# A two-layer latent trunk on one core: h summed in DRAM by the DMA, g stored from GpSimd, layer 0's gate columns computed in the first stage, and a new order of the loop's pieces

## The chip, the cores and the metric

The kernel runs on one core of one Trainium2 chip. The metric is the device time of one execution in microseconds, the median of three runs. A profile of one execution comes with each kernel; its times count from the first instruction.

## What is computed

Two residual layers over 1024 latent tokens and 256 context tokens, width 1024, in float32. Layer 0 is a bidirectional gated linear recurrence (RG-LRU) of width 1408, layer 1 a windowed attention. The change lies in layer 0:

```
def modulation(vec, w, b):
    m = jax.nn.silu(vec) @ w + b
    shift, scale, gate = jnp.split(m, 3, axis=-1)
...
    a = jnp.exp(log_a)
    b = jnp.sqrt(-jnp.expm1(2.0 * log_a)) * (i * uf)
...
    h_l = hl_dirs[0] + hl_dirs[1]
    y_l = (h_l * jax.nn.silu(g_l.astype(jnp.float32))).astype(n_l.dtype) @ w_out
...
        h_lat = h_lat + gt_l * y_l
```

Here u and g are the two halves of n @ w_in, u goes through a convolution over four tokens, r and i are sigmoids of products of u with 16 block matrices of 88x88 for each direction, and each direction is a linear scan over the tokens, with the context first. The two directions' h are added, multiplied by silu(g) and projected.

## The kernel before

Channels lie on partitions, the 1280 tokens in the free dimension, in three token tiles of 512, 512 and 256 (CH). Float32 products are made of three passes over a rounded part and a remainder (mm3, lines 76 to 78), so each operand is split in two: the rounded part mostly by ScalarE, the remainder mostly by VectorE.

The program fixes the order of every engine by hand (a manual schedule). Two tables of short names set it: `sorder` for the first stage (loads, norm, modulation, u of the first two channel tiles) and `order` for the loop over the rest. An entry such as `U3.1.0` is one half of the product of u tile 3 with token tile 1; each engine and each DMA queue runs its own entries in the table's order, and waits only where data or a buffer is missing.

The names in the loop: W loads half a weight tile, wh and wl split it; U and G are products for u and g (G over 11 tiles t, three token tiles, two halves of 12 matmuls); c1 and tp the convolution; ub copies blocks of u to 88 partitions, uh and ul split them; Q is the product for the gates of block b, in three parts of nine matmuls, into one PSUM tile `gtps`; sg its sigmoid into a tile M (two buffers); pc moves M's rows by DMA to the channel tiles R (for r) and I (for i), z = 0 forward and 1 reverse, four buffers each. Then, for each channel tile (chain) j and direction z: tn, ex and sq (tanh, exp, square root, ScalarE), iu, m1, m2 (VectorE), and sc, the scan, which writes over I. `ad` adds the two directions on VectorE (ch_add, line 524) and `hs` stores the sum to h_dr in DRAM (line 527). `ev` copies a G product from its bank (two banks) into the one buffer ev_g, and `gs` stores it to g_dr (line 612). All DMAs are issued by SyncE, in the table's order. GpSimd does next to nothing in the loop.

The last entries, once all gates are done, are the drain. Into it the program places loads for what follows: three tiles of h and g (og_load, lines 744 and 745), and gate columns of layer 0 (ada_w0g, 4 MB): ad_load, ad_mm (16 products of 32x512, line 551), ad_row (line 556) and ad_tr (four transposes, line 562, and the adds into gate0). Then the output projection runs (names c and wh_j, wl_j; GpSimd makes wl_j at line 70): it multiplies h by silu(g) in tiles (og_prep, line 750), which og_load keeps four ahead.

Of the kernel before, what the change touches and what calls it, by code (L numbers as in the profile page):

```python
# [8 lines left out]
F32 = mybir.dt.float32  # L9
# [26 lines left out]
def trunk(ctx: ExitStack, tc: tile.TileContext, I, out, dbg=None, stop=None):  # L36
# [155 lines left out]
    sel2 = px.tile([P, 2], F32, name="sel2")  # L192
    nbn = px.tile([P, KD], F32, name="nbn")
# [90 lines left out]
    def ada0_row(b):  # L284
        arow[b] = px.tile([P, 256], F32, tag="arow", name=f"arow0_{b}", bufs=1)
        act.copy(arow[b], aps[b][:, :256])
# [63 lines left out]
    dve.tensor_reduce(sel2, ident.rearrange("p (j r) -> p r j", j=4)[:, 0:2, :], op=ALU.add, axis=mybir.AxisListType.X)  # L350
    lam_b()
# [3 lines left out]
    def diag(i):  # L355
# [20 lines left out]
    uo = {i: [a[1] for f, a in sorder if f == "U" and a[0] == i] for i in range(3)}
    lasta = max(n for n, (f, _) in enumerate(sorder) if f == "am")
# [239 lines left out]
    def c_tap(k, x):  # L617
# [151 lines left out]
    def ogx(i, k):  # L769
# [811 lines left out]
```

## Time and profile before

| | us |
|---|---|
| runs before | 1262.64, 1263.79, 1263.93 |
| median | 1263.79 |
| the profiled execution | 1264.06 |
| its span, first to last instruction | 1262.2 |
| TensorE busy | 1186.7 (94%) |
| VectorE busy | 759.1 (60%) |
| ScalarE busy | 726.7 (58%) |
| GpSimd busy | 467.3 (37%) |

TensorE is busy nearly throughout. The span is not one stage: the first stage, the loop with its drain, the output projection, layer 1's products, its attention and its projection follow each other, and each has its own limit. A busy share says little on a change that lies in one of them; the stretch and its waits have to be read. Matmuls overlap, so the distance between two starts, not the duration of one, is what a matmul costs.

### The profile page before, as it was taken

To read this page: it belongs to the slowest core of one execution; us is meant where nothing else is said; L and a number is where in the kernel's file an instruction comes from. 1 tells how busy PE (TensorE), PEld (TensorE's weight loads), DVE (VectorE), ACT (ScalarE), POOL (GpSimd) and SP (SyncE) were. 2 spreads that over 40 slices of the span, in tenths; PEclk is the share of its full clock that TensorE was granted. 3 is DMA by queue.
4 is the path that set the end of the run, shared out by engine and by line. 5 is a ranking of instruction groups with operands and counts; after the bars stand their busy time and mean duration, and the time that the engine had idled before them with its cause. 6 is when DMAs were issued, how large, how long until landed. Compare 5 with 4: busy or idle time off the path is not lost. (4 is left out here: it accounts for less than half of the span.)

```text
span 1262.2 us, 18495 instructions
## 1 busy us (share of the span) xinstructions
PE 1186.7 (94%) x6702; PEld 975.9 (77%) x6702; DVE 759.1 (60%) x1185; ACT 726.7 (58%) x1163; POOL 467.3 (37%) x528
## 2 busy tenths in 40 slices
PE   8999999999987878889999999999999999999997
PEld 7788878878775756767788888777778887876787
DVE  3763958677686375643055735530069999996343
ACT  5656878677696465641022545631179999985212
POOL 3000000000000002454547545553248888898722
PEclk9999989999998889999999999999999999999998
DMA  9435565646555666968516457789482442211422
GB/s 351 157 90 165 159 188 156 166 125 187 137 160 149 174 241 218 328 210 290 180 55 226 168 173 226 219 246 321 137 260 65 169 142 89 85 34 43 142 84 68
DMA packets 96653, 214.02 MB, mean 170 GB/s; under 512 B 10290, under 2 KB 23986, under 8 KB 94514
## 3 DMA queue, kind: packets, MB, share of 16 engines
q1 hardware_dynamic: 96562, 212.84, 53.6%
q8 instruction: 53, 0.87, 0.3%
q14 instruction: 38, 0.31, 0.1%
HBM read 127.73 MB, written 49.02 MB: 140 GB/s over the span
## 5 line engine op out<-in xcount | busy, mean ns | idle before, releaser
L70 POOL TENSOR_TENSOR wl_j<-ws_j,wh_j 128x512 fp32r<-128x512 f32 (+1 forms) x94 | 127.4, 1359 | 461.6 <-ACT wh_j L717 447.0
L1182 DVE CUSTOM_DVE_ANT_0 p<-s,mask,snk 128x640 f32<-128x640 f32 (+1 forms) x128 | 106.7, 837 | 23.8 <-PE s L1171 23.5
L1202 POOL TENSOR_SCALAR p<-p,den 128x640 f32<-128x640 f32 (+1 forms) x128 | 98.6, 793 | 59.5 <-DVE den L1198 45.7
L76 PE MATMUL g<-n0h,wh 128*128 128x512 f32 (+1 forms) x264 | 99.3, 376 | 15.1 <-ACT ev_g L608 13.9
L1188 ACT ACTIVATE p<-p,nm 128x640 f32<-128x640 f32 (+1 forms) x128 | 102.7, 804 | 1.2 <-DVE nm L1182 1.1
L77 PE MATMUL g<-n0h,wl 128*128 128x512 f32 (+1 forms) x264 | 98.5, 373 | 0.0
L78 PE MATMUL g<-n0l,wh 128*128 128x512 f32 (+1 forms) x264 | 97.4, 369 | 0.0
L1214 PE MATMUL t<-ident,p 128*128 128x128 f32 x608 | 92.9, 276 | 2.6 <-DVE tl L1229 2.0
L1214 PEld LDWEIGHTS t<-ident,p 128*128 128x128 f32 x608 | 72.3, 141 | 27.3 <-DVE tl L1229 12.5
L76 PE MATMUL u<-n0h,wh 128*128 128x512 f32 (+1 forms) x240 | 87.0, 363 | 3.4 <-DVE uc L414 3.4
L77 PE MATMUL u<-n0h,wl 128*128 128x512 f32 (+1 forms) x240 | 85.9, 358 | 0.0
L78 PE MATMUL u<-n0l,wh 128*128 128x512 f32 (+1 forms) x240 | 85.5, 356 | 0.0
L1229 DVE TENSOR_TENSOR tl<-t,th 128x512 fp32r<-128x512 f32 x120 | 82.2, 687 | 1.9 <-ACT th L1221 1.1
L471 ACT ACTIVATE M<-gtps,pack 128x1280 f32<-128x1280 f32 (+1 forms) x48 | 63.7, 1327 | 29.6 <-PE gtps L78 26.2
L67 POOL TENSOR_SCALAR wh_j<-ws_j 128x512 fp32r<-128x512 f32 (+1 forms) x72 | 51.9, 720 | 70.7 <-DMA ws_j<-w_in1t 25.7
L1221 ACT CAST th<-t 128x512 fp32r<-128x512 f32 x120 | 70.4, 587 | 11.5 <-PE t L1214 7.8
L77 PE MATMUL c<-n0h,wl_j 128*128 128x512 f32 x192 | 69.9, 364 | 2.7 <-POOL wl_j L70 2.7
L76 PE MATMUL c<-n0h,wh_j 128*128 128x512 f32 x192 | 70.2, 366 | 2.0 <-ACT wh_j L717 2.0
L76 PEld LDWEIGHTS g<-n0h,wh 128*128 128x128 f32 x264 | 53.2, 201 | 24.2 <-ACT ev_g L608 15.8
L78 PE MATMUL c<-n0l,wh_j 128*128 128x512 f32 x192 | 68.9, 359 | 0.0
L76 PE MATMUL gtps<-uh,gh 88*128 88x512 f32 (+1 forms) x144 | 53.9, 374 | 14.5 <-ACT M L471 14.4
L1169 PE MATMUL s<-kst,qa 128*128 128x256 f32 x256 | 59.6, 314 | 4.1 <-DVE nm L1182 2.9
(447 smaller groups left out, 3429.6 us busy)
## 6 DMA issues: line engine op xcount, KB each, us to landing
qa<-x_dr SPq DMA_DIRECT2D x16, 1024.0 KB
aw<-ada_w SPq DMA_DIRECT2D x48, 256.0 KB
ws_j<-w_in1t SPq DMA_DIRECT2D x48, 256.0 KB
ws<-w_in0t SPq DMA_DIRECT2D x44, 256.0 KB
adaw<-ada_w0c SPq DMA_DIRECT2D x16, 512.0 KB
x_dr<-h_q SPq DMA_DIRECT2D x32, 256.0 KB
x_dr<-l_q SPq DMA_DIRECT2D x32, 256.0 KB
h_dr<-I SPq DMA_DIRECT2D x11, 640.0 KB
```

What stands on the lines that cost most here:

```text
L70: pool.tensor_tensor(d, a, b, op=ALU.subtract)
L76: pe.matmul(ps, wh, xh, start=first, stop=False)
L77: pe.matmul(ps, wl, xh, start=False, stop=False)
L78: pe.matmul(ps, wh, xl, start=False, stop=last)
L471: act.activation(t[:rows], d.pop(("ps", m))[:rows, :T], AF.Sigmoid, bias=gbias[:rows, b, m:m + 1])
L1169: pe.matmul(ps[:, 256:512], qp, kst[:, z, NL:], start=(z == 0), stop=(z == 1))
L1182: dve.tensor_tensor_reduce(p, ps[:, 256:256 + nk], msk, 1.0, snk[:, h:h + 1], ALU.add, ALU.min, d["nm"][:, hh:hh + 1])
L1188: act.activation(p, p, AF.Exp, bias=d["nm"][:, hh:hh + 1], scale=-1.0, accum_out=d["den"][:, hh:hh + 1])
L1202: pool.tensor_scalar(d["p"][hh], d["p"][hh], d["den"][:, hh:hh + 1], 1.0, op0=ALU.mult, op1=ALU.mult)
L1214: pe.transpose(tp[:, y * P:(y + 1) * P], d["p"][hh][:, x * P:(x + 1) * P], ident)
L1221: act.copy(d["h", i], d["t", i])
L1229: dve.tensor_tensor(d["l", i], d["t", i], d["h", i], op=ALU.subtract)
```

## The change

`ad` and `hs` go. In their place stand `hx`, a plain store of the reverse direction's I to h_dr, and `hy`, a DMA that adds the forward direction's I to the same rows of h_dr; both are issued by GpSimd, as are the g stores now. Gate columns of layer 0 are computed in the first stage: gd loads a 128x1024 part of ada_w0g, gm makes four of the 16 products, gr copies the rows, gt turns them into columns with a selection matrix (four products with four columns), gc adds the bias. The drain's ada pieces go, and six h and g tiles in place of three are loaded in it. Both tables are new; of each a line or two is shown.

```
+    sel4 = px.tile([P, 4], F32, name="sel4")
...
+    def gd(t):
+        w = araw["g", t] = pw.tile([P, 1024], F32, tag="adaw", name=f"adawg{t}", bufs=8)
+        nc.sync.dma_start(w, I["ada_w0g"][t * P:(t + 1) * P, :])
+
+    def gm(q):
+        if q == 0:
+            aps["g"] = gt("adapsg")
+        for a in range(2):
+            for h in range(2):
+                pe.matmul(aps["g"][64 * a + 32 * h:64 * a + 32 * h + 32], scc[:, 2 * q + a, :],
+                          araw["g", 2 * q + a][:, 512 * h:512 * h + 512], start=(q == 0), stop=(q == 3))
+
+    def g_row(_):
+        arow["g"] = px.tile([P, 512], F32, tag="arow", name="arowg", bufs=1)
+        act.copy(arow["g"], aps["g"])
+
+    def g_tr(_):
+        for c in range(4):
+            pe.matmul(aps["g"][:, 4 * c:4 * c + 4], arow["g"][:, c * P:(c + 1) * P], sel4, start=True, stop=True)
+
+    def g_col(_):
+        pc = aps["g"][:, 0:16].rearrange("p (c h r) -> p h c r", h=2, r=2)
+        for h in range(2):
+            hs = slice(4 * h, 4 * h + 4)
+            dve.tensor_tensor(gate0[:, hs, :], pc[:, h], ada_b0[:, 2 * KD:3 * KD].unsqueeze(2).to_broadcast([P, KD, 2])[:, hs], op=ALU.add)
...
-        ev0.0 l2.7 U2.2 U2.7 ev0.2 ev1.2
...
+        U2.2 wl2.0 ev0.1 U2.4 ev1.1 U2.0 h2.7 U2.1 wh2.1 l2.7 gr0 U2.7 wl2.1 gt0 ev1.2 ev0.2 gc0
...
-    lasta = max(n for n, (f, _) in enumerate(sorder) if f == "am")
+    lasta = max(n for n, (f, _) in enumerate(sorder) if f in ("am", "gm"))
...
-    def ch_add(j):
-        c = chn[j]
-        dve.tensor_tensor(c["I", 0], c["I", 0], c["I", 1], op=ALU.add)
-
-    def hstore(j):
-        nc.sync.dma_start(h_dr[j * P:(j + 1) * P, :], chn.pop(j)["I", 0])
+    def hstore1(j):
+        pool.dma_start(h_dr[j * P:(j + 1) * P, :], chn[j]["I", 1])
+
+    def hstore0(j):
+        pool.dma_start(h_dr[j * P:(j + 1) * P, :], chn.pop(j)["I", 0], accum_op=ALU.add)
...
-        nc.sync.dma_start(g_dr[t * P:(t + 1) * P, c0:c0 + n], evg.pop((t, i)))
+        pool.dma_start(g_dr[t * P:(t + 1) * P, c0:c0 + n], evg.pop((t, i)))
...
-        m110.1 ev9.1 G10.2.1 gs9.1 m210.1 G9.2.0 sc10.1 G9.2.1 ev10.2 gs10.2 ad10 hs10 ev9.2 gs9.2
...
+        m29.1 G9.2.1 ex10.0 sc9.1 sq10.0 hx9 ev9.2 m110.0 gs9.2 m210.0 sc10.0 hy10 ev10.2 gs10.2 hy9
...
-    hq0 = adE.enter_context(pl_(name="hq0", bufs=3, side="right"))
+    hq0 = adE.enter_context(pl_(name="hq0", bufs=6, side="right"))
...
-    og_load(0, 0)
-    ad_load(2)
-    og_load(0, 1)
-    ad_load(6)
-    og_load(0, 2)
-    lastg = [n for n, (f, _) in enumerate(order) if f == "G"][-4]
...
+    left = len(order) - lastu - 1
+    ogat = {lastu + 1 + (q + 1) * left // 8: q for q in range(6)}
     for n, (f, a) in enumerate(order[lastu + 1:], lastu + 1):
-        if n == lastg:
-            ad_mm(0)
-            ad_load(8)
+        if n in ogat:
+            og_load(0, ogat[n])
         loop[f](*a)
...
-    for q in range(1, 4):
-        ad_mm(q)
...
-    ogn = [3, 0]
+    ogn = [6, 0]
```

SyncE's queue where the gates of block 15 come, before (R1_10 is the reverse direction's R of chain 10, M15_0 the first part of block 15's gates, ev_g7_0 a G product):

```order
L485 DMA R1_10_3466<-M15_0_3449 88x1280
L485 DMA R0_10_3468<-M15_0_3449 40x1280
L612 DMA g_dr_61<-ev_g7_0_3473 128x512
L485 DMA R0_10_3468<-M15_1_3476 48x1280
L485 DMA I1_10_3494<-M15_1_3476 80x1280
L612 DMA g_dr_61<-ev_g7_1_3506 128x512
L485 DMA R1_9_3302<-M14_0_3524 48x1280
L485 DMA R1_10_3466<-M14_0_3524 40x1280
L485 DMA R0_9_3305<-M14_0_3524 40x1280
L172 DMA ws21_0_3556<-w_in0t 128x512
L612 DMA g_dr_61<-ev_g7_2_3558 128x256
```

and after:

```order
L515 DMA R1_10_3542<-M15_0_3510 88x1280
L515 DMA R0_10_3544<-M15_0_3510 40x1280
L515 DMA R0_10_3544<-M15_1_3588 48x1280
L515 DMA I1_10_3605<-M15_1_3588 80x1280
L515 DMA I1_10_3605<-M15_2_3635 8x1280
L515 DMA I0_10_3650<-M15_2_3635 88x1280
L172 DMA ws20_1_3662<-w_in0t 128x512
L172 DMA ws21_0_3666<-w_in0t 128x512
L515 DMA R1_9_3359<-M14_0_3669 48x1280
```

The three g stores between the pieces are gone from this queue, and block 15's last part stands ahead of block 14's first.

GpSimd's queue at the end of the loop, before (uc0 is the first convolution, wl_j0 the projection's first weight remainder):

```order
L268 TENSOR_SCALAR sp8_117<-lam_0_119 128x22
L406 TENSOR_SCALAR uc0_861<-ev0_665,pack_62 128x1280
L70 TENSOR_TENSOR wl_j0_3965<-ws_j0_3776,wh_j0_3964 128x512
L70 TENSOR_TENSOR wl_j1_3975<-ws_j1_3778,wh_j1_3974 128x512
L70 TENSOR_TENSOR wl_j2_4009<-ws_j2_3780,wh_j2_4008 128x512
```

and after (the DMA of I1 is the plain h store, that of I0 the accumulating one):

```order
L553 DMA h_dr_60<-I1_10_3605 128x1280
L641 DMA g_dr_61<-ev_g9_1_3913 128x512
L553 DMA h_dr_60<-I1_9_3393 128x1280
L641 DMA g_dr_61<-ev_g9_2_3961 128x256
L556 DMA h_dr_60<-I0_10_3650 128x1280
L641 DMA g_dr_61<-ev_g10_2_3969 128x256
L556 DMA h_dr_60<-I0_9_3438 128x1280
L70 TENSOR_TENSOR wl_j0_3984<-ws_j0_3843,wh_j0_3983 128x512
```

Where nothing stood between the first convolution and the projection there are now 55 stores, and the last of them stand ahead of wl_j0.

VectorE at the end of the drain, before (chains 9 and 10; t2 is the product's tile):

```order
L507 SCALAR_TENSOR_TENSOR t2_10_0_3774<-R0_10_3468,t2_10_0_3774 128x1280
L524 TENSOR_TENSOR I0_9_3388<-I0_9_3388,I1_9_3340 128x1280
L511 TENSOR_TENSOR t2_10_0_3774<-t2_10_0_3774,I0_10_3620 128x1280
L517 SCALAR_TENSOR_TENSOR I0_10_3620<-R0_10_3468,t2_10_0_3774 128x256
L518 SCALAR_TENSOR_TENSOR I0_10_3620<-R0_10_3468,I0_10_3620,t2_10_0_3774 128x1024
L507 SCALAR_TENSOR_TENSOR t2_10_1_3832<-R1_10_3466,t2_10_1_3832 128x1280
L511 TENSOR_TENSOR t2_10_1_3832<-t2_10_1_3832,I1_10_3494 128x1280
L520 SCALAR_TENSOR_TENSOR I1_10_3494<-R1_10_3466,t2_10_1_3832 128x1280
L524 TENSOR_TENSOR I0_10_3620<-I0_10_3620,I1_10_3494 128x1280
```

and after (oh0_0 is the projection's first h tile):

```order
L537 SCALAR_TENSOR_TENSOR t2_9_1_3889<-R1_9_3359,t2_9_1_3889 128x1280
L541 TENSOR_TENSOR t2_9_1_3889<-t2_9_1_3889,I1_9_3393 128x1280
L550 SCALAR_TENSOR_TENSOR I1_9_3393<-R1_9_3359,t2_9_1_3889 128x1280
L537 SCALAR_TENSOR_TENSOR t2_10_0_3934<-R0_10_3544,t2_10_0_3934 128x1280
L541 TENSOR_TENSOR t2_10_0_3934<-t2_10_0_3934,I0_10_3650 128x1280
L547 SCALAR_TENSOR_TENSOR I0_10_3650<-R0_10_3544,t2_10_0_3934 128x256
L548 SCALAR_TENSOR_TENSOR I0_10_3650<-R0_10_3544,I0_10_3650,t2_10_0_3934 128x1024
L778 TENSOR_TENSOR oh0_0_3852<-oh0_0_3852,sg0_0_3853 128x512
```

The two additions (L524) are gone, the forward direction of chain 10 is last, and the reverse direction of chain 9 stands right ahead of it.

## Rows read from the trace of the kernel before

**Rows 1.** Busy time by stretches: us, then PE, PEld, DVE, ACT, POOL, granted clock, DMA, GB/s.
```profile
140.00:160.00 20.00, 20.00 (x104) 17.11 (x103) 16.22 (x15) 19.11 (x18) 0.00 (x0) 1.00 0.57 164
...
400.00:420.00 20.00, 10.94 (x36) 8.43 (x34) 16.27 (x12) 10.46 (x10) 0.00 (x0) 0.74 0.20 52
...
520.00:540.00 20.00, 18.53 (x80) 14.46 (x78) 12.83 (x16) 12.47 (x23) 7.96 (x7) 1.00 0.97 360
```

**Rows 2.** Waits of SyncE's queue, 380 to 487 us: total, times, longest.
```profile
SPq L485 <- DVE I L520: 17.3, 1, 17.3
```

**Rows 3.** Timeline of SyncE's queue, 380 to 470 us: start, duration of the issues, line.
```profile
393.73 2.00 SPq L485 DMA_DIRECT2D I<-M  x3
413.06 3.68 SPq L485 DMA_DIRECT2D R<-M  x2
416.84 0.43 SPq L612 DMA_DIRECT2D g_dr<-ev_g  x1
...
462.19 7.49 SPq L612 DMA_DIRECT2D g_dr<-ev_g  x2
```

**Rows 4.** Timeline of TensorE: start, duration, operation, in brackets the idle time before.
```profile
395.52 0.39 PE L77 MATMUL g<-n0h,wl 128*128 128x512 f32 x1
395.74 0.39 PE L78 MATMUL g<-n0l,wh 128*128 128x512 f32 x1
...
407.08 0.80 PE L76 MATMUL gtps<-uh,gh 88*128 88x512 f32 x1 [5.79 <-ACT M L471]
...
408.53 0.63 PE L76 MATMUL gtps<-uh,gh 88*128 88x512 f32 x1
408.96 0.63 PE L77 MATMUL gtps<-uh,gl 88*128 88x512 f32 x1
...
421.54 0.58 PE L76 MATMUL g<-n0h,wh 128*128 128x256 f32 x1 [4.82 <-ACT ev_g L608]
...
440.49 0.28 PE L78 MATMUL gtps<-ublk,gh 88*96 88x256 f32 x1
...
493.21 0.77 PE L76 MATMUL c<-n0h,wh_j 128*128 128x512 f32 x1
```

**Rows 5.** Timeline of ScalarE, the copies of G products.
```profile
408.60 0.58 ACT L608 COPY ev_g<-g 128x512 f32<-128x512 f32 x1
...
420.90 0.59 ACT L608 COPY ev_g<-g 128x512 f32<-128x512 f32 x1 [8.84 <-DMA g_dr<-ev_g]
...
468.74 0.59 ACT L608 COPY ev_g<-g 128x512 f32<-128x512 f32 x1 [10.07 <-DMA g_dr<-ev_g]
```

**Rows 6.** VectorE's groups by shape, 380 to 488 us: busy, mean ns, idle before.
```profile
L511 DVE TENSOR_TENSOR t<-t,I 128x1280 f32<-128x1280 f32 x6 | 8.8, 1487 | 0.1
...
L520 DVE TENSOR_TENSOR_SCAN I<-R,t 128x1280 f32<-128x1280 f32 x3 | 8.5, 2818 | 0.0
L518 DVE TENSOR_TENSOR_SCAN I<-R,I,t 128x1024 f32<-128x1024 f32 x3 | 7.1, 2351 | 0.1
```

**Rows 7.** ScalarE's groups by shape, 380 to 488 us.
```profile
L495 ACT ACTIVATE R<-R,sp 128x1280 f32<-128x1280 f32 x6 | 8.1, 1362 | 0.1
...
L499 ACT ACTIVATE t<-t 128x1280 f32<-128x1280 f32 x6 | 7.7, 1276 | 0.1
...
L499 ACT ACT_TABLE_LOAD x5 | 6.4, 1283 | 0.1
```

**Rows 8.** Timeline of TensorE, the products for the gate columns.
```profile
477.86 1.07 PE L551 MATMUL adaps<-aw,scc 128*32 128x512 f32 x8
...
484.80 2.78 PE L551 MATMUL adaps<-aw,scc 128*32 128x512 f32 x24
```

**Rows 9.** Waits of TensorE, 493 to 620 us: total, times, longest.
```profile
PE c L77 <- POOL wl_j L70: 4.3, 5, 1.0
```

**Rows 10.** Waits of ScalarE, 487 to 560 us.
```profile
ACT sg L750 <- DMA sg<-g_dr: 18.4, 9, 3.5
```

**Rows 11.** Waits of TensorE in the loop up to 340 us.
```profile
PE gtps L76 <- ACT M L471: 7.1, 5, 2.4
```

More of the change, by code (lines that the diff above doesn't have):

```diff
@@ L284, in ada0_row @@
     def ada0_row(b):
-        arow[b] = px.tile([P, 256], F32, tag="arow", name=f"arow0_{b}", bufs=1)
+        arow[b] = px.tile([P, 512], F32, tag="arow", name=f"arow0_{b}", bufs=1)[:, :256]
         act.copy(arow[b], aps[b][:, :256])
@@ L350, in trunk @@
     dve.tensor_reduce(sel2, ident.rearrange("p (j r) -> p r j", j=4)[:, 0:2, :], op=ALU.add, axis=mybir.AxisListType.X)
+    dve.tensor_reduce(sel4.rearrange("p (h r) -> p h r", h=2),
+                      ident.rearrange("p (a h r) -> p h r a", a=2, h=2)[:, :, 0:2, :], op=ALU.add, axis=mybir.AxisListType.X)
     lam_b()
@@ new lines, in trunk @@
+        am3.0 y0.0 h1.0 U1.1 A5.0 wh1.1 l1.0 h0.0 am3.1 wl1.1 A4.1 U1.0 row3 l0.0 A2.1 tr3 am4.0 col3
+        U0.0 y1.3 W0.1 y0.3 h1.3 A2.0 am5.0 h0.3 l1.3 am4.1 am5.1 row4 l0.3 A6.0 U1.3 wh0.1 A6.1 tr4
+        wl0.1 U0.3 col4 row5 y1.4 X2.0 y0.4 tr5 h1.4 am2.0 W2.1 col5 l1.4 am2.1 h0.4 am6.0 A7.0 y0.5
+        U1.4 row2 l0.4 h0.5 A7.1 y1.5 sq2.0 tr2 am6.1 l0.5 U0.4 W2.0 col2 h1.5 y1.2 X2.1 am7.0 row6 y0.2
+        pq2.0 h1.2 tr6 l1.5 U0.5 h0.2 gd4 l1.2 col6 l0.2 U1.2 gd3 y1.6 sq2.1 y0.6 U1.5 gd5 h0.6 h1.6
@@ new lines, in trunk @@
+        ev1.2 wl13.1 gs1.2 sc0.0 gw4 W4.1 Q2.2 gh3 G2.0.1 sg2.2 gl3 pc2.1 hy0 tp3.0 gh4 tn1.1 gl4 Q3.0
+        W5.0 tp3.1 W14.0 ev2.0 wh4.1 gs2.0 G2.1.0 sq1.1 wl4.1 tp3.2 gw5 G2.1.1 ex1.1 ub4 iu1.1 pc2.2
+        sg3.0 U4.0.0 m11.1 m21.1 ev2.1 pc3.0 U4.0.1 tn1.0 gs2.1 sc1.1 uh4 Q3.1 sq1.0 ul4 hx1 U4.1.0
+        iu1.0 sg3.1 U4.1.1 ex1.0 pc3.1 Q3.2 m11.0 U4.2.0 sg3.2 m21.0 U4.2.1 sc1.0 wh14.0 pc3.2 Q4.0 c14
+        G2.2.0 sg4.0 wl14.0 hy1 G2.2.1 tp4.0 gh5 pc4.0 wh5.0 Q4.1 ev2.2 wl5.0 gs2.2 gl5 tp4.1 G3.0.0
@@ new lines, in trunk @@
+        W14.1 sg4.1 W5.1 gw6 tp4.2 pc4.1 Q4.2 ub5 U5.0.0 wh14.1 wh5.1 wl14.1 gh6 wl5.1 W6.0 tn2.1 gl6
+        ub6 G3.0.1 W15.0 sg4.2 W6.1 sq2.1 pc4.2 U5.0.1 iu2.1 ev3.0 ex2.1 gs3.0 G3.1.0 tn2.0 m12.1 G3.1.1
+        uh5 m22.1 ex2.0 ul5 U5.1.0 ev3.1 sq2.0 sc2.1 gs3.1 Q5.0 uh6 m12.0 hx2 G3.2.0 sg5.0 ul6 G3.2.1
+        iu2.0 U5.1.1 wh6.1 pc5.0 ev3.2 wl6.1 gs3.2 m22.0 Q5.1 sc2.0 U5.2.0 sg5.1 U5.2.1 wh6.0 wh15.0
+        wl6.0 pc5.1 hy2 Q5.2 wl15.0 c15 tp5.0 G4.0.0 tn3.1 gw7 gw8 sg5.2 W15.1 tp5.1 sq3.1 Q6.0 tp5.2
@@ new lines, in trunk @@
+        wh16.0 gs4.2 sq4.0 wl16.0 W8.0 ex4.1 U7.1.1 ex4.0 m14.1 G5.0.0 sg7.2 m14.0 U7.2.0 m24.1 uh9
+        pc7.2 Q8.0 sc4.1 U7.2.1 sg8.0 ul9 hx4 G5.0.1 pc8.0 wh8.1 wh8.0 wl8.1 wl8.0 Q8.1 ev5.0 gs5.0
+        iu4.0 G5.1.0 sg8.1 m24.0 c17 Q8.2 sc4.0 G5.1.1 gh9 sg8.2 gl9 pc8.1 hy4 tp7.0 tn5.1 Q9.0 ev5.1
+        tp7.1 sq5.1 gs5.1 G5.2.0 W17.0 gw10 tp7.2 gw11 G5.2.1 ex5.1 U8.0.0 ub10 gh10 m15.1 wh17.0 U8.0.1
+        ev5.2 gs5.2 gl10 sg9.0 pc8.2 wl17.0 iu5.1 G6.0.0 W17.1 m25.1 tn5.0 pc9.0 uh10 sc5.1 gw12 Q9.1
@@ new lines, in trunk @@
+        ex5.0 U8.1.0 ul10 hx5 sg9.1 iu5.0 U8.1.1 sq5.0 pc9.1 Q9.2 wh17.1 m15.0 U8.2.0 sg9.2 wl17.1
+        U8.2.1 m25.0 gh11 pc9.2 Q10.0 sc5.0 c18 G6.0.1 sg10.0 tp8.0 pc10.0 hy5 Q10.1 ev6.0 gl11 gs6.0
+        tp8.1 G6.1.0 W9.1 sg10.1 W9.0 tp8.2 pc10.1 Q10.2 ub11 G6.1.1 gh12 wh9.1 gl12 wh9.0 wl9.1 gw13
+        wl9.0 sg10.2 gw14 ub12 U9.0.0 ev6.1 W10.0 tn6.0 pc10.2 gs6.1 tn6.1 U9.0.1 iu6.1 uh11 ex6.1 ul11
+        G6.2.0 U9.1.0 sq6.1 iu6.0 Q11.0 sq6.0 m16.1 U9.1.1 sg11.0 m26.1 sc6.1 G6.2.1 ex6.0 Q11.1 pc11.0
@@ new lines, in trunk @@
+        hx6 ev6.2 m16.0 U9.2.0 sg11.1 gs6.2 U9.2.1 m26.0 wh10.0 Q11.2 sc6.0 c19 gh13 uh12 wl10.0 ul12
+        pc11.1 hy6 tn7.1 gl13 tp9.0 sg11.2 tp9.1 sq7.1 Q12.0 W10.1 tp9.2 ex7.1 U10.0.0 ub13 wh10.1 m17.1
+        sg12.0 pc11.2 wl10.1 iu7.1 U10.0.1 m27.1 tn7.0 pc12.0 Q12.1 uh13 sc7.1 sq7.0 U10.1.0 ul13 hx7
+        sg12.1 U10.1.1 iu7.0 ex7.0 pc12.1 Q12.2 U10.2.0 sg12.2 m17.0 U10.2.1 m27.0 gh14 Q13.0 pc12.2
+        c110 gl14 sc7.0 W19.0 W18.1 sg13.0 W19.1 Q13.1 tp10.0 pc13.0 hy7 tp10.1 wh19.0 wh18.1 sg13.1
@@ L731, in trunk @@
     adE, ogE = ExitStack(), ExitStack()
-    adp = adE.enter_context(pl_(name="adp", bufs=1, side="right"))
-    ad_load, ad_mm, ad_row, ad_tr = ada_stream(adp, (0,), 6, lambda nm: ps6.tile([P, 512], F32, tag="a", name=nm),
-                                             lambda nm: adp.tile([P, 512], F32, tag="row", name=nm))
-    hq0 = adE.enter_context(pl_(name="hq0", bufs=3, side="right"))
+    hq0 = adE.enter_context(pl_(name="hq0", bufs=6, side="right"))
     ogc, ogs = {}, {}
```

97 lines of the change are left out of this document (33 added, 64 removed).

## The prediction, made before the changed kernel ran

> **What bounds the kernel now.** I read the busy time by stretches first, then TensorE's own idle gaps in the timeline, then what SyncE's queue and ScalarE waited for at the same moments, and last the durations by shape, for the sums. The first stage, the loop and the drain end when the output projection starts, at 493.21 us of the span [rows 4]; what lies behind it isn't touched. Up to there TensorE is the engine that is nearly always busy, 20.00 of 20 us in a good stretch, at the full granted clock; at 400 to 420 us it is busy for 10.94 with a mean granted clock of 0.74 [rows 1]. So a change here pays where it takes TensorE's gaps away, and VectorE's or SyncE's time is worth nothing by itself.
>
> The two gaps of that stretch are 5.79 us before a gate product (its PSUM tile waits for the sigmoid, M) and 4.82 us before a G product (its bank waits for ev_g) [rows 4]. Behind the first gap matmuls of 512 columns start 0.43 us apart in place of 0.22 [rows 4]: the granted clock is at its lower level there, 1.2 of 2.4 GHz. Both gaps come from SyncE: one of its issues, a piece of block 15, waited 17.3 us for a buffer of the R ring (released by the reverse scan of chain 8) [rows 2], from 395.73 to 413.06 [rows 3]. Behind it in the same queue stood the other pieces, so both M buffers stayed full, and the g store of the copy at 408.60, issued only at 416.84 [rows 3, 5]. With one ev buffer the next copy waited 8.84 us for that store to land [rows 5]. In the drain the same happens again: the copy at 468.74 waited 10.07 us for a store that SyncE began to issue at 462.19, behind loads of the gate columns and weights [rows 3, 5].
>
> **The change part by part.** The sum is made against the profiled run, 1264.06 us; the median of the three runs, 1263.79, lies 0.27 below it, which is less than anything here.
>
> *Gate columns in the first stage: +4.5 us there.* The sixteen products (32 records of 128x512) take 1.07 us for eight and 2.78 for 24 [rows 8], 3.85 together. At their old place only the first 1.07 lay between G products; the rest ran where TensorE then waited anyway. In the first stage TensorE has no gap after the first products of u, so all of it counts, with some 0.6 for four small products that turn the row into columns. Their 4 MB of loads go out behind the first stage's own; the products stand late in that stage, so I take no wait for them (bound: 2 us). ScalarE's copy and VectorE's two adds stand at the end of the stage, hidden by the U2 products; uncovered they cost 1.
>
> *Scan directions summed by the DMA.* VectorE loses eleven additions of 1.49 us, the size of the other 128x1280 operations [rows 6], in the loop off the path: 0. What it costs is on GpSimd's queue: 22 h stores and 33 g stores in one order, and each accumulating store waits there for the scan of its own direction and for the plain store of the same rows to land, with g stores behind it. GpSimd issues no DMA in this trace. From below its price is SyncE's issue row, 0.43 us for a g store [rows 3]; from above a landing of a g store, 4.1 us (416.84 to 420.90) or 6.5 (462.19 to 468.74) [rows 3, 5]. With 0.58 for the copy, 0.43 and 4.1, evacuations follow each other every 5.1 us, and a G piece of 24 matmuls at 0.22 or 0.23 takes 5.4 with a second bank ahead. So I take 0 for the loop, because the loop's DMA engines are less loaded than at 462.19, where the 6.5 stands, and keep 22 us for the range (rival A).
>
> The Trainium skill (DMA: Bandwidth & Descriptors, Specifications) puts the first byte of a DMA from GpSimd at about 1 us, against 0.6 from SyncE. No row here shows it, since GpSimd issues none. By it the evacuations would be estimated at 5.5 us apart and the three last stores on GpSimd at 1.2 us more, so 1246 for the whole.
>
> *g stores off SyncE's queue, and the new order around chains 8 to 10: -14.7.* The after-order still issues block 15's first pieces before the scans of chain 8, so SyncE blocks there again; but no g store stands behind it, and between the gate products of block 15 now stand G8.2, G7.0, G7.1 and G7.2: 16 us of work. ScalarE and VectorE need for chain 8 from the first gate of block 15 on: six vector operations of 1.49 or 2.8 with two activations and table loads, some 14.5 us [rows 6, 7], so M is free before TensorE runs out. The two gaps go, 5.79 and 4.82, with the slow matmuls behind: fifteen of 512 and three of 256 columns at 0.2 and 0.1 each, 3.3, and about 2.5 behind the second. That is 16.4. One hand-over appears (gates 14.0 and 14.1 stand next to each other; a sigmoid of 1.3 and its way lie between): 1.7 back.
>
> *More TensorE work before the last gate: +5.6.* Before, four pieces of 512 columns (24 matmuls, 5.45 us) and three of 256 (2.83) followed the last gate: 30.3 us. After it, three and a half of the one and two of the other: 24.7. What is not behind is ahead.
>
> *From the last gate to the projection: -11.6.* Before it is 440.6 to 493.21, 52.6 us [rows 4]. After, counted from the last gate's end at 0: sigmoid until 1.6, pieces landed about 4.3. ScalarE then runs in order tanh, exp, sqrt for 10.1, then for 9.0, 9.1 and 10.0, each 1.28 to 1.36 with eight table loads of 1.28 [rows 7] and the copies between: square root of 9.1 done at 23.1, of 10.0 at 30.2. VectorE: products for 9 and 10 until 16.2, scan 10.1 (2.82) to 19.0, 9.0 to 25, multiplications and scan for 9.1 to 30.8, for 10.0 (1.49, 1.49, then 2.35 and about 0.7) to 36.8 [rows 6]. GpSimd then has the accumulating store of 10, a g store, the accumulating store of 9 and the first weight subtraction, four steps of about 1 us: 41. The oldest part of the projection's data (n0h, n0l of tile 0) is ready at about the same time: ScalarE is free at 35.5. So 41 in place of 52.6. TensorE is then idle for some 14 us; the drain is bound by VectorE and ScalarE.
>
> *Six og tiles loaded ahead instead of three, no gate loads in the drain: -3.* The projection's first products waited 4.3 us for GpSimd's wl_j, because ScalarE stood 18.4 us for loads of sg [rows 9, 10]. 1.5 MB less to load there is about 4 us at the 360 GB/s of the stretch 520 to 540 [rows 1]; half to all of it shows at TensorE, I take 3. None of it (0) if the first wh_j is the later one.
>
> Sum: 4.5 - 14.7 + 5.6 - 11.6 - 3 = -19.2, and 1264.06 - 19.2 = 1244.9.
>
> **The rivals.** *A, slower: GpSimd's queue takes SyncE's place.* An accumulating store moves 640 KB and reads as much back; if it, or the load that it puts on the engines, makes the g stores land at 6.5 us, as at 462.19, evacuations come every 7.5 us against 5.4 and TensorE stands 2.05 us at one hand-over per G tile: 11 x 2.05 = 22.6, with some 3 us more for the three stores ahead of the first wl_j: 1270. From 1.75 us per tile on (19.2 / 11) the gain is gone. For it: ev has one buffer, and a stall costs the clock too. Against: only eight G pieces follow a G piece directly in the new order, the others have other work between.
>
> The Trainium skill (DMA: Bandwidth & Descriptors, Rules for kernel authors) says that spreading DMAs over SyncE, ScalarE and GpSimd doesn't help, since all run on the same 16 engines, and saves issue time only. The trace shows both shares: at 420.90, 7.7 us in the queue and 4.1 after the issue [rows 3, 5]. By that rule the second share would stay or grow, which is this rival.
>
> *B: the ring wait stays a stall.* If SyncE's block at block 15 again leaves M full (chain 8 late by more than 2 us), the 14.7 stay: 1259.6. For it: the same pieces wait for the same scans.
> *C: nothing is left.* B, and a drain that gets shorter only by the work that moved out of it (5.6 instead of 11.6): 1259.6 + 6 = 1265.6.
> *D: more goes.* The gaps before 340 us, 7.1 for M [rows 11] and about as much low clock behind them, go with the freed SyncE queue, and so does the 1.3 that I leave of the projection's 4.3: 1244.9 - 14.2 - 1.3 = 1229.4.
>
> **How the numbers follow.** The forecast, 1234 to 1256, has 0.50; B 0.17, A 0.16, D 0.10, C 0.07. The bounds of the forecast are those of its terms: loop start 2 to 6.5, gaps 10 to 20, drain 5 to 14, projection 0 to 7. The range 1229 to 1268 leaves out most of A and half of D, some 0.18. A measurement can tell about 0.2%, 2.5 us, from no change: faster 0.77 (forecast, D, nearly all of B), same 0.07, slower 0.16.
>
> **What would show it.** The projection's first product should start near 474 us; the first loop product 4 to 5 us later than before; no TensorE gap above 3 us between 340 and the last gate; the last gate to the projection about 41 us with VectorE's chain of 18 operations unbroken; GpSimd's issues about 1 us each, and ev_g's waits for g stores under 2 us. Wrong would be: many short gaps of G products waiting for ev_g (A), SyncE's long wait with M behind it and TensorE idle at once (B), or a first stage that ends over 7 us later.

## The result, and the profile after

The changed kernel took 1281.27 us in the median (1280.48 to 1284.1) against 1263.22 (1261.85 to 1263.93) for the kernel before on the same chip: a ratio of 1.0147, interval 1.0133 to 1.0161. It is 18 us slower, where 19 us faster was forecast, and it lies outside the forecast range of 1229 to 1268. The profiled execution took 1284.1 us, 20.0 more than the one of before.

Busy time by stretches, after; the columns are those of [rows 1], to which two of these lines answer (440 to 460 is new):

```profile
400.00:420.00 20.00, 18.25 (x78) 14.40 (x77) 8.97 (x9) 13.47 (x14) 1.10 (x2) 0.87 0.61 147
440.00:460.00 20.00, 7.29 (x20) 5.33 (x21) 1.39 (x2) 5.45 (x6) 1.43 (x2) 0.57 0.67 159
520.00:540.00 20.00, 15.61 (x61) 12.21 (x60) 11.19 (x17) 12.39 (x22) 9.09 (x6) 0.91 0.85 296
```

The hole of 400 to 420 us is nearly closed (18.25 us busy in place of 10.94), and a deeper one has opened 40 us later: 7.29 us busy at a mean granted clock of 0.57, that is, mostly at the lower level of 1.2 GHz. TensorE's timeline after, to be set against [rows 4]:

```profile
336.83 0.80 PE L76 MATMUL u<-n0h,wh 128*128 128x512 f32 x1 [5.64 <-ACT wh L611]
...
441.55 0.50 PE L76 MATMUL gtps<-uh,gh 88*128 88x512 f32 x1 [3.14 <-ACT M L501]
...
445.96 0.80 PE L76 MATMUL gtps<-uh,gh 88*128 88x512 f32 x1 [1.72 <-ACT M L501]
...
458.96 0.80 PE L76 MATMUL g<-n0h,wh 128*128 128x512 f32 x1 [9.43 <-ACT wh L611]
...
465.51 0.28 PE L78 MATMUL gtps<-ublk,gh 88*96 88x256 f32 x1
...
504.71 0.80 PE L76 MATMUL c<-n0h,wh_j 128*128 128x512 f32 x1 [9.71 <-ACT n0h L63]
507.09 0.79 PE L77 MATMUL c<-n0h,wl_j 128*128 128x512 f32 x1 [1.58 <-POOL wl_j L70]
510.08 0.80 PE L78 MATMUL c<-n0l,wh_j 128*128 128x512 f32 x1 [2.19 <-DVE n0l L64]
```

In the whole loop TensorE stood 17.7 us for the casts of weights (wh), in three gaps (2.65 us in one near 193, 5.64 and 9.43); in the kernel before that was 1.2 us in one.

From such lines every kernel below is cut into four pieces: the start of the loop (the first product of u with the weights wx), the loop from there to the end of the last gate product, from there to the first product c, and from that to the last product c. In us:

| kernel | loop starts at | loop to last gate | last gate to projection | projection |
|---|---|---|---|---|
| before | 69.3 | 371.5 | 52.4 | 177.1 |
| after | 74.0 | 391.8 | 38.9 | 185.7 |
| difference | +4.7 | +20.3 | -13.5 | +8.6 |

The four differences make 20.1, the whole loss. By the prediction's estimate the new order does 5.6 us of TensorE's work ahead of the last gate that was behind it, so some 14.7 of the 20.3 are a real loss.

What stood in the way at 449 to 459 us is in SyncE's queue (first its waits from 380 to 487 us, to be read beside [rows 2]; then its timeline) and in GpSimd's timeline:

```profile
SPq L515 <- DVE I L548: 17.7, 1, 17.7
SPq L515 <- DMA h_dr<-I: 13.2, 2, 8.4
```
```profile
425.34 10.62 SPq L515 DMA_DIRECT2D R<-M  x3
440.76 10.80 SPq L515 DMA_DIRECT2D I<-M  x3
451.61 2.11 SPq L172 DMA_DIRECT2D ws<-w_in0t  x2
```
```profile
434.79 0.54 POOL L553 DMA_DIRECT2D h_dr<-I  x1 [2.25 <-DVE I L550]
442.27 0.54 POOL L641 DMA_DIRECT2D g_dr<-ev_g  x1 [6.94 <-ACT ev_g L637]
442.84 0.89 POOL L556 DMA_DIRECT2D h_dr<-I  x1
```

The pieces of block 15 wait for chain 8 as before, first for R (the last of these pieces is out at 435.96). Then they wait for I buffers, 13.2 us in all: 4.8 until 440.76 for one that the plain store of 434.79 still reads, and 8.4 more for one that the adding store of 442.84 still reads. In the kernel before SyncE waits for no such buffer. No g store stands behind them now, but weight loads do: ws goes out at 451.61, and ScalarE's cast of it waited 11.57 us:

```profile
457.48 0.62 ACT L611 CAST wh<-ws 128x512 fp32r<-128x512 f32 x1 [11.57 <-DMA ws<-w_in0t]
```

ScalarE's waits for landings from the loop's start to the last gate (total, times, longest), after:

```profile
ACT wh L611 <- DMA ws<-w_in0t: 33.8, 10, 11.6
...
ACT ev_g L637 <- DMA g_dr<-ev_g: 6.7, 4, 5.4
```

and before:

```profile
ACT wh L582 <- DMA ws<-w_in0t: 19.1, 8, 4.6
...
ACT ev_g L608 <- DMA g_dr<-ev_g: 11.0, 2, 8.8
```

The copies of G wait less for g stores, the casts of weights much more for their loads.

At the start of the projection (GpSimd, VectorE, SyncE, ScalarE, in this order):

```profile
503.41 0.88 POOL L556 DMA_DIRECT2D h_dr<-I  x1 [5.37 <-DVE I L548]
503.98 0.87 POOL L641 DMA_DIRECT2D g_dr<-ev_g  x1
504.52 1.22 POOL L556 DMA_DIRECT2D h_dr<-I  x1
505.11 4.35 POOL L70 TENSOR_TENSOR wl_j<-ws_j,wh_j 128x512 fp32r<-128x512 f32 x3
```
```profile
500.76 2.35 DVE L548 TENSOR_TENSOR_SCAN I<-R,I,t 128x1024 f32<-128x1024 f32 x1
...
504.79 5.23 DVE L64 TENSOR_TENSOR n0l<-oh,n0h 128x512 fp32r<-128x512 f32 x1
```
```profile
507.06 9.22 SPq L736 DMA_DIRECT2D ws_j<-w_out  x4
```
```profile
513.93 0.62 ACT L746 CAST wh_j<-ws_j 128x512 fp32r<-128x512 f32 x1 [7.71 <-DMA ws_j<-w_out]
```

VectorE's last scan ends at 503.11, 37.3 us behind the last gate's end (465.79). The three weight subtractions stand behind GpSimd's last three stores; until they are done SyncE has no buffer for the next weights, which go out from 507.06 on.

### The profile page after: what moved, and what is told of

Same layout as the page of the kernel before. It is cut to its first block, busy times and chain, and to the rows that moved or that the text cites. A ratio compares the mean times of both kernels' runs of the same rounds, so it can differ in the third digit from the quotient of the medians.

```text
span 1282.3 us, 18596 instructions
## 1 busy us (share of the span) xinstructions
PE 1187.0 (93%) x6706; PEld 973.7 (76%) x6706; DVE 745.5 (58%) x1173; ACT 733.2 (57%) x1168; POOL 499.6 (39%) x583
## 3 DMA queue, kind: packets, MB, share of 16 engines
HBM read 127.73 MB, written 56.23 MB: 143 GB/s over the span
## 5 line engine op out<-in xcount | busy, mean ns | idle before, releaser
L641 POOL DMA_DIRECT2D g_dr<-ev_g x33 | 18.5, 561 | 246.0 <-ACT ev_g L637 237.3
L76 PE MATMUL g<-n0h,wh 128*128 128x512 f32 (+1 forms) x264 | 96.8, 367 | 14.7 <-ACT wh L611 12.1
```

Of the source, the lines that this page charges most:

```text
L76: pe.matmul(ps, wh, xh, start=first, stop=False)
```

## The experiments

Theory 1: the accumulating stores cost it (1a by holding the I buffers, 1b by their load on the DMA engines). Theory 2: the new order does, by the weight loads behind block 15's pieces. Theory 3: GpSimd's queue in front of the projection. All ratios are to the kernel before on the same chip, with the 95% interval; 0.1% is 1.26 us, and differences between two kernels are taken from their ratios. Where the intervals of two kernels overlap, their difference isn't clear of the noise. The last four columns are cut as above, in us.

| kernel | ratio | loop starts | loop | to projection | projection |
|---|---|---|---|---|---|
| after | 1.0147 (1.0133 to 1.0161) | 74.0 | 391.8 | 38.9 | 185.7 |
| a1: after, sum on VectorE | 1.0034 (1.0017 to 1.0051) | 73.8 | 379.3 | 40.9 | 178.5 |
| a2: after, weight loads ahead | 1.0119 (1.0088 to 1.0149) | 73.8 | 386.9 | 40.2 | 185.5 |
| a3: after, early splits | 1.0123 (1.009 to 1.0157) | 73.7 | 391.1 | 41.3 | 177.7 |
| c1: a1, a2 and a3 together | 1.0013 (0.9992 to 1.0035) | 73.7 | 374.5 | 45.7 | 179.6 |
| a6: after, narrow adding stores | 0.9997 (0.9973 to 1.0022) | 73.7 | 369.7 | 38.9 | 181.7 |
| a8: a1, adding stores to scratch | 1.022 (1.0191 to 1.0249) | 73.7 | 394.3 | 40.9 | 179.6 |
| a9: a1, plain stores to scratch | 1.0055 (1.0039 to 1.0072) | 73.7 | 379.3 | 40.8 | 179.2 |
| b1: before, accumulating stores | 1.0177 (1.0149 to 1.0205) | 69.6 | 382.3 | 62.1 | 177.3 |
| b1n: before, narrow adding stores | 0.9957 (0.9938 to 0.9976) | 69.2 | 366.7 | 52.9 | 180.4 |
| b2: before, g stores on GpSimd | 0.9939 (0.9916 to 0.9963) | 69.3 | 365.6 | 46.9 | 178.1 |
| b3: before's loop, new ends | 0.9946 (0.9928 to 0.9964) | 73.7 | 371.5 | 38.1 | 179.4 |
| b4: b3, g stores on GpSimd | 0.9957 (0.9936 to 0.9979) | 74.2 | 368.1 | 43.0 | 178.6 |
| d1: b4, h stores on GpSimd | 0.9958 (0.9942 to 0.9975) | 73.7 | 368.0 | 42.0 | 181.1 |

The pieces are those of one profiled run for each kernel, and that run can lie some us off the median (b2 and a8 5 below, c1 5 above, after 3 above), so small differences between pieces are no more than hints.

**Undoing the sum by DMA (a1).**

```diff
+    def hsum(j):
+        c = chn.pop(j)
+        dve.tensor_tensor(c["I", 0], c["I", 0], c["I", 1], op=ALU.add)
+        pool.dma_start(h_dr[j * P:(j + 1) * P, :], c["I", 0])
...
     def hstore0(j):
-        pool.dma_start(h_dr[j * P:(j + 1) * P, :], chn.pop(j)["I", 0], accum_op=ALU.add)
+        if j != 9:
+            hsum(j)
```

The first direction's own store (hx) goes; for chain 9 alone the sum stands at that store's place.

> The changed kernel with the sum of the scan directions back on VectorE and one plain store per chain from GpSimd; order, g stores and first stage stay. In the changed kernel SyncE waits 10.8 us (440.8 to 451.6) for the buffer I of chain 8 that the accumulating store of 442.8 still reads, with weight loads behind it. Theory 1 (the accumulating stores hold the I buffers): that wait falls to under 3 us, the gap of 9.4 us in front of the first G10 product shrinks by as much, and the whole falls by 6 to 12 us to about 1272; the sum adds 1.5 us in the drain. Theory 2 (the new order puts weight loads behind block 15's pieces, whatever stores h): the wait shrinks by 2 to 4 us, as the add stands at the late place of the second store, 1278 to 1282.

14 of the 18 us were gone, more than the 6 to 12 that theory 1 had set. By the pieces of the profiled runs: 12.5 in the loop, 7.2 in the projection, 2.0 given back in the drain.

**The same store in the kernel before (b1).** Each scan is followed by GpSimd's store of its direction, the second one adding; the add and SyncE's h store go.

```diff
+        pool.dma_start(h_dr[j * P:(j + 1) * P, :], c["I", z], **({} if first else dict(accum_op=ALU.add)))
```

> The kernel before with only the accumulating stores: each direction of a chain is stored by GpSimd right behind its scan, the second one adding; no VectorE add; order, g stores on SyncE and gate columns as before. Theory 1 (accumulating stores hold I buffers longer): SyncE's waits for I grow, 1268 to 1275. Theory 2 (the order is at fault): 1260 to 1265, with VectorE's eleven adds gone and nothing on the path.

22 us slower in the old order too (a median of 1285.1, where theory 1 had 1268 to 1275). Theory 2 alone is out: the accumulating stores cost more than the whole loss of the change. But SyncE's waits for I buffers that a store still reads, which theory 1 wants longer, came to 2.3 us only up to the last gate.

**Weight loads ahead (a2) and early splits (a3), the two stalls that the trace of after shows.**

```diff
-        Q15.0 iu8.0 G8.2.0 ...
+        W20.1 W21.0 W21.1 Q15.0 iu8.0 G8.2.0 ...
```

At their old places, behind block 15, the three entries are taken out.

> The changed kernel with three weight loads (20.1, 21.0, 21.1) issued ahead of block 15's first gate and pieces, nothing else moved. Theory 2 (head of line in SyncE's queue): the 11.6 us in which ScalarE waits for ws at 445 to 457 go, and with them TensorE's gap of 9.4 us and the 2 us of low clock behind it: about 1270. Theory 1 (accumulating stores hold the buffers): the pieces of block 15 still wait until 451.6, so the last gate is late all the same, TensorE only does its G10 work ahead of it; the drain after the last gate is 39 us whatever it holds, and the gain is under 4 us: 1277 to 1281.

TensorE's gap of 9.43 us went, but the last gate then waited for M (TensorE, then SyncE in that run):

```profile
457.10 0.74 PE L76 MATMUL gtps<-uh,gh 88*96 88x512 f32 x1 [3.31 <-ACT M L501]
```
```profile
440.74 9.66 SPq L515 DMA_DIRECT2D I<-M  x3
```

The last gate ended 5 us earlier. The ratio fell by 3.5 us (1.0147 to 1.0119), but the intervals overlap, so of the whole this run shows only that the gain is small, as theory 1 had it: with the weights there, the pieces are late all the same.

```diff
+        if (f, a) == ("hy", (10,)):
+            wsplit(2)
         loop[f](*a)
```

> The changed kernel with the projection's first three weight splits (casts on ScalarE, subtractions on GpSimd) put ahead of GpSimd's accumulating store of chain 10 and not behind the three last stores. Theory 3 (GpSimd's queue delays the subtractions, so SyncE can load the next weights only at 507 and ScalarE and TensorE wait for them): SyncE's 28 us wait for wl_j falls below 10, the gaps of 1.6, 2.2 and 3.4 us at 507, 510 and 526 go, 6 to 8 us: about 1274. Rival (the projection waits for og data, gates loaded too late): 1280 to 1282. It gets slower if GpSimd's subtractions slow the last scan on VectorE: up to 4 us, 1285.

The projection took 177.7 us in place of 185.7: theory 3's stall is real, and its 8 us went. But 2.4 were given back ahead of it, and the ratios differ by 3 us only, with intervals that overlap; the median of 1279.5 lies between the two expectations. GpSimd's subtractions now ran beside VectorE's last chain (GpSimd, then VectorE):

```profile
497.08 5.61 POOL L70 TENSOR_TENSOR wl_j<-ws_j,wh_j 128x512 fp32r<-128x512 f32 x3
```
```profile
497.53 2.44 DVE L541 TENSOR_TENSOR t<-t,I 128x1280 f32<-128x1280 f32 x1
500.00 1.64 DVE L547 TENSOR_TENSOR_SCAN I<-R,t 128x256 f32<-128x256 f32 x1
501.67 3.17 DVE L548 TENSOR_TENSOR_SCAN I<-R,I,t 128x1024 f32<-128x1024 f32 x1
```

The product takes 1.49 us otherwise and the second part of the scan 2.35 [rows 6]; its first part took 0.69 one chain earlier in this run. In the changed kernel itself one split of 0.68 us took 5.23 beside GpSimd's 4.35 (above). The Trainium skill (SBUF — State Buffer, Who interferes with whom) says that a VectorE instruction with two inputs in SBUF contends with a GpSimd instruction that reads SBUF; these rows agree.

**All three mends (c1).**

> The changed kernel in its new order with the three mends together: sum on VectorE, the three weight loads ahead of block 15, the first weight splits ahead of the last stores. Alone they gave 14, 3.5 and 4 us. If they add: 1259 to 1261. If the first two mend the same stall (SyncE behind block 15): 1263 to 1265.

1.0013, a median of 1263.3: the second expectation. By the ratios that is 2.6 us on top of a1, with intervals that overlap. The three mends overlap too, and the new order with all of them is no faster than the kernel before.

**Hold or load (a6, a7, a8, a9, b1n).** a6 and b1n leave the place and the waits of the adding stores as they are and let them write 64 of 1280 columns; the rest of the sum is left out:

```diff
-        pool.dma_start(h_dr[j * P:(j + 1) * P, :], chn.pop(j)["I", 0], accum_op=ALU.add)
+        pool.dma_start(h_dr[j * P:(j + 1) * P, :64], chn.pop(j)["I", 0][:, :64], accum_op=ALU.add)
```

> The changed kernel, but the adding store of each chain writes 64 of 1280 columns (the other columns of the sum are left out); its place, its wait for the plain store and the two plain stores' sizes stay. With the sum on VectorE the changed kernel took 1267, so the adding stores cost about 14 us. Theory 1a (the cost is the hold of the I buffer by the place and the wait in GpSimd's queue): the buffer of chain 8 is still released only at about 448, 1277 to 1282. Theory 1b (the cost is the bytes: 640 KB more per chain that land late and delay pieces and weight loads): 1264 to 1270, near the kernel with the sum on VectorE.

a8 does the opposite. To a1 it adds a store of full size that holds no I buffer; a9 makes the same store a plain one:

```diff
         pool.dma_start(h_dr[j * P:(j + 1) * P, :], c["I", 0])
+        if j < 9:
+            pool.dma_start(scr, nsrc, accum_op=ALU.add)
```

Here scr is a block in DRAM and nsrc 1280 columns of n0h, which the loop only reads; one plain store of nsrc stands ahead of the loop.

> As the run with the adding store beside VectorE's sum, but the source is 1280 contiguous columns, so the rows of the store (5 KB) are those of the accumulating store; in the earlier run they were 640 bytes, eight times as many, so that run's 25 us over the kernel with the sum on VectorE (1267) overstate the bytes. Theory 1b (bytes, at about twice the DMA time of plain ones): 1273 to 1282, most of the 14 us. Theory 1a (hold of I): 1265 to 1270.

> As the run with an adding store of 640 KB per chain beside VectorE's sum (1288), but the extra store is a plain one into the same scratch block: the same bytes without the addition. If an adding store costs more than a plain one of its size (in the queue table 11 adding stores took about 36 us of all 16 engines, 11 plain ones about 20): 1273 to 1280. If the bytes alone count: 1284 to 1290. If the earlier run's cost was the hold in some form: 1265 to 1268.

> The kernel before with accumulating stores (1285 in full), but the adding store of each chain writes 64 of 1280 columns; the other columns of the sum are left out. Theory 1b (the bytes of the adding stores): 1256 to 1264, at or under the kernel before. Theory 1a (hold by the place in GpSimd's queue and its wait for the first store): over 1275.

a6 was 19 us faster than after (0.9997 against 1.0147), b1n 28 faster than b1. a8 was 23 us slower than a1 without touching an I buffer; a9 only 3 slower (the intervals overlap), with the same bytes. (a7, the first form of a8 with rows of 640 bytes in place of 5 KB, gave 1.0242, 26 over a1; its median of 1293 is above both readings.)

> The kernel with the sum on VectorE (1267), with an adding store of 640 KB per chain beside it for chains 0 to 8, from a tile that is never rewritten in the loop into a scratch block: the bytes of the accumulating store, without a hold of the I buffers by it. Theory 1b (bytes): 1275 to 1283. Theory 1a (hold): 1265 to 1270.

a6 and b1n came out where theory 1b had them or below. a8 overshot it (1288), and a9 (1269) fell well under both readings by bytes, next to the one by a hold (1265 to 1268). But what a9 leaves out of a8 is the addition alone, and neither scratch store reads a buffer that the loop waits for. SyncE's waits for I buffers that a store still reads, up to the last gate (total, times, longest), in a8 and a9:

```profile
SPq L515 <- DMA h_dr<-I: 5.1, 1, 5.1
SPq L515 <- DMA h_dr<-I: 4.6, 1, 4.6
```

They are nearly the same, and between b1 (2.3) and b1n (0.3) they differ by 2 us, where the kernels are 28 apart. So the addition is what costs, far more than the bytes or the hold. The pages of a8 and a9 show it in the time of GpSimd's queue (packets, MB, share of 16 engines) and in the row of the scratch stores (count, KB, median us to landing). a8:

```profile
q0 software_dynamic: 5312, 20.97, 5.8%
scr<-n0h POOLq DMA_DIRECT2D x10, 640.0 KB, 10.0
```

and a9:

```profile
q0 software_dynamic: 5312, 20.97, 4.5%
scr<-n0h POOLq DMA_DIRECT2D x10, 640.0 KB, 7.2
```

and a1 without them:

```profile
q0 software_dynamic: 3872, 14.42, 3.3%
```

The ten plain stores of a9 thus took 1.5 us of all 16 engines each (4.5% of 1266.8 us less 3.3% of 1263.4, by ten). In a8 the first of the ten is plain, too, and the nine that add took 3.5 each (5.8% of 1280.8 less 41.7 and 1.5, by nine). What the others then wait: ScalarE's waits for its g stores and for weights to land, up to the last gate (total, times, longest), a8:

```profile
ACT wh L624 <- DMA ws<-w_in0t: 30.3, 11, 9.4
ACT ev_g L650 <- DMA g_dr<-ev_g: 19.8, 5, 10.1
```

and a9:

```profile
ACT wh L624 <- DMA ws<-w_in0t: 24.9, 11, 8.7
ACT ev_g L650 <- DMA g_dr<-ev_g: 8.6, 3, 6.9
```

Over all rows of that kind ScalarE waited 43 to 67 us for landings in the kernels without full adding stores (from a6 43.3, b1n 46.0 and before 56.8 up to b4 65.1 and d1 67.1), and 75 to 80 with them (from a3 74.8, a8 75.9 and after 76.8 to b1 80.0). The total alone doesn't set the time: d1 waits longer than the kernel before and is faster. But from a9 to a8, which differ in nothing else, it is 20 us more, in a loop that took 15.0 us longer. The five g stores that GpSimd issued within 2.3 us behind a scratch store landed after 6.2 to 9.9 us in a9 and after 8.7 to 13.0 in a8. And the two runs part step by step: GpSimd's h store of chain 0 starts at the same time in both (149.9), that of chain 4 6.0 us later in a8 (293.3 against 287.3), that of chain 8 13.9 (447.6 against 433.7).

**The other parts alone (b2, b3, b4, d1).** b2 changes one line, `nc.sync` to `pool` in `g_st`.

> The kernel before with only its g stores issued by GpSimd (one line). ScalarE's waits for g stores, 25.3 us in all, should shrink to under 12, the TensorE gap of 4.8 us near 422 goes and the drain's copy no longer waits 10 us for a store: 5 to 12 us faster, 1251 to 1258. Rival: block 15's pieces still hold SyncE, both M buffers and TensorE, so the gaps stay; 1260 to 1264.

7.7 us faster, within the first expectation. Of the two gaps of [rows 4] the second is gone and the first is 1 us shorter; one of 2.46 us for M, which the kernel before doesn't have, stands near the place of the second:

```profile
405.54 0.80 PE L76 MATMUL gtps<-uh,gh 88*128 88x512 f32 x1 [4.84 <-ACT M L471]
419.62 0.50 PE L76 MATMUL gtps<-uh,gh 88*128 88x512 f32 x1 [2.46 <-ACT M L471]
```

b3 keeps the loop of before (table, VectorE's sum, stores on SyncE) between the changed first stage and drain.

> The loop of the kernel before (its order, VectorE's sum, all stores on SyncE) between the changed first stage and the changed drain: gate columns in the first stage, no gate loads in the drain, six og tiles loaded ahead. First stage 4.6 us longer. If the gate loads (4 MB at 450 to 470) were what delayed the drain's g stores, the drain gets 5 to 10 us shorter: 1255 to 1262. Rival: the drain was bound elsewhere: 1265 to 1268.

6.8 us faster, within the first expectation, with 38.1 us from the last gate to the projection in place of 52.4. The copy that waited 10.07 us at 468.74 [rows 5] did not wait in this run:

```profile
467.58 0.56 ACT L638 COPY ev_g<-g 128x512 f32<-128x512 f32 x1
```

b4 is both, d1 has the h stores on GpSimd as well.

> The loop of the kernel before in its old order with g stores from GpSimd, between the changed first stage and drain; sum on VectorE, h stores on SyncE: the change without the accumulating stores and without the new loop order. Alone the g stores gave 6 us and the ends 7. If the two add up: about 1249. If the freed drain is the same time counted twice: 1253 to 1256. Against the changed kernel with the sum on VectorE (1267) the rest is the new order of the loop: 10 to 18 us.

> The loop of the kernel before in its old order, with VectorE's sum, g and h stores both from GpSimd, between the changed first stage and drain. From the changed kernel with the sum on VectorE (1265) it differs by the loop's order alone, from the run with h stores on SyncE (1256) by the queue of eleven h stores alone. If the new order costs: 1253 to 1258. If h stores on GpSimd cost: 1262 to 1267.

The two gains do not add (0.9957): b4's median of 1256.3 comes next to its second expectation, 0.3 us above its end. Both take away the one wait of 10.1 us for a g store in the drain (the longest is 3.7 in b2, 2.9 in b3 and 4.2 in b4), but in all ScalarE waited there for g stores 14.2 us before, 14.6 in b2, 6.5 in b3 and 10.0 in b4; why b4 keeps more of that than b3, and a drain 4.9 us longer, no run shows. d1 is the same (0.9958), so h stores on GpSimd cost nothing that the noise would show. From d1 to a1 only the order of the loop changes, with the place of the sum in it: 1.0034 against 0.9958, 9.6 us slower by the new order. (In a1 the sum stands at the late place of the second store, for which the order wasn't made; a6, which has no addition on VectorE, is still 4.9 us behind d1, with intervals that just touch.)

## Why the prediction was wrong, step by step

The forecast of -19.2 and the +20.1 of the profiled run are 39.3 us apart. By the four pieces 29.4 of them lie in the loop (+5.6 less 14.7 was forecast, +20.3 came) and 11.6 at the projection (-3 forecast, +8.6 came); the other two pieces make -1.7.

- *First stage +4.5*: 4.7. Right.
- *Scan directions summed by the DMA, 0 in the loop*: this is the step that failed. It measured 14 us (after against a1) with VectorE's adds paid back, 19 with a narrow store in its place (a6), 28 in the old order (b1 against b1n). The step bounded the store by GpSimd's issue and by the landing of a g store, and took the lower bound, as "the loop's DMA engines are less loaded". The sum did not ask what the addition does to the transfers of others. Rival A did: it had the sign and nearly a size (1270), and named a read-back. But in the changed kernel it put the wait at the wrong place: the waits of the copies for g stores in the loop fell from 11.0 to 6.7 us, and the weight loads paid instead, 33.8 us of waiting in place of 19.1. In a8, against a9, both grew, and the g stores' share more (8.6 to 19.8 and 24.9 to 30.3). The step's other 0, for VectorE's additions off the path, may be off as well: without them a6 is 4.7 us faster than a1, and b1n 5.4 faster than the kernel before; but both change the stores too.
- *Gaps around chains 8 to 10, -14.7*: half right. The 16 us of work between block 15's gates do cover chain 8 (18.25 us busy in place of 10.94 from 400 to 420 us), and the hand-over between gates 14.0 and 14.1 costs 1.72, where the step had 1.7. What it missed stands around that: 3.14 us for M ahead of 14.0, and 9.43 ahead of G10's first product, whose weights stood behind block 15's pieces. The step looked for g stores behind SyncE's blocked pieces and found none; it did not look for the weight loads that the new table puts there, nor for the I buffers that the stores hold. The g stores alone are worth 5.9 us in the loop (b2). Less the 5.6 of moved work, the loop of the new order is 7.4 us shorter than before without full adding stores (a6: 364.1 against 371.5), and 2.2 longer with the sum on VectorE (a1: 373.7).
- *More work before the last gate +5.6*: right; behind the last gate TensorE worked from 465.8 to 495.0 with one gap of 2.63 us, and about 1.6 us of it are the price of matmuls at the lower clock (256 columns 0.21 us apart in place of 0.12): some 25 against the 24.7 of the step.
- *Last gate to projection -11.6*: -13.5. The size was right, and so was the path up to VectorE's last scan: it ends 37.3 us behind the last gate, where the step had 36.8. The 4 us behind it for GpSimd's stores were not there: the first product came 1.6 us after the scan. But the new order wasn't needed for it: b3 reaches 38.1 with the old one and its longer tail. What left the drain in b3 is the gate columns, their loads and products, and the prediction had put the loads into the next step.
- *Six og tiles, no gate loads, -3 at the projection*: +8.6. No run shows the -3: b3, which has both, takes 179.4 us there against 177.1 before. GpSimd's last stores, which the step before had counted as 1 us each ahead of the first product, also stand ahead of three subtractions, and so of SyncE's next weight loads. a3 shows it: 177.7 with the subtractions ahead. a1, with two of the h stores less in the tail, has 178.5.
- *GpSimd's issue about 1 us*: 0.54 for a plain store, 0.88 for one that adds. GpSimd's queue was not the bound of the loop: of the 246 us that it stood idle ahead of its g stores it waited 237 for the copies. As to the figure of the Trainium skill (DMA: Bandwidth & Descriptors, Specifications) for the first byte, no row here shows it.
- *The rule that several issuing engines save issue time only* (Trainium skill, DMA: Bandwidth & Descriptors, Rules for kernel authors): b2 shows one thing more. It changes only the engine that issues the g stores, and with it their place in a queue, and that place was worth 0.6% here: the stores no longer stand behind a waiting piece, as the one did for which a copy waited 8.84 us at 420.90 [rows 5].

The sum of what the runs give: the ends and the g stores together -5.4 us (b4), the h stores on GpSimd 0 (d1), the new order +9.6 (a1), the addition in the DMA +14.3 (after). That is +18.5; it adds up by construction, since each term is a difference between two neighbouring kernels. b2 (ratio 0.9939) and b3 (0.9946) beat the kernel before and the changed one.

**Open.** The plain scratch stores cost the kernel 0.3 us each, the adding ones 2.6 (2.6 and 23.5 us by the ratios), for 1.5 and 3.5 us of engine time; why the second part of that time costs so much more than the first, the rows do not say. A read-back isn't seen either: the pages of a8 and a9 count the same 127.73 MB read from HBM. A hold of the I buffers without any load was not run by itself. SyncE's waits for them bound it: 13.2 us in the changed kernel, 8.2 in a6 and 4.6 in a1, so that some of the changed kernel's loss may be the longer hold by the slower store, while in a8 and b1 there is hardly any. Where the new order loses its 9.6 us is only partly known: in a1 TensorE still stands 6.34 us ahead of G10's first product, and the 2.6 us that c1's two further mends took off are not clear of the noise.

## What to carry to other kernels

Work that is moved from an idle engine into the DMA isn't free because the engine's time was: ask what else is in flight on the same DMA engines and who waits for it to land, and test the store alone before building an order around it. When a queue's blocked instruction stays where it is, list everything that the new program puts behind it, not only what stood there before. Changes made together should be run apart: two parts of this one were worth 0.5 to 0.6% each and were buried under a third.

## What the runs showed of the hardware

- A store of 640 KB that adds took 3.5 us of all 16 DMA engines, a plain one 1.5; the medians to landing were 10.0 and 7.2 us (a8, a9). The kernel lost about 2.6 us for each of the first and 0.3 for each of the second, which isn't clear of 0.
- Nine stores that add in place of nine plain ones lengthened ScalarE's waits for other transfers by 20 us (55.9 to 75.9), weight loads of SyncE's queue among them (24.9 to 30.3).
- GpSimd issues a plain store in 0.54 us and an adding one in 0.88.
- VectorE's instructions stretched while GpSimd subtracted: from 1.49 to 2.44 us and from 2.35 to 3.17 (a3), and one from 0.68 to 5.23 (after).
